# Encoder layer on one core: the sums move from GpSimd to VectorE, ten block pairs run two at a time, and six stores of the output add to a row stored early

## The chip, the cores and the metric

The kernel runs on one core of a Trainium2 chip. The metric is the device time of one execution in microseconds (us); the time before is the median of three runs. The engines are TensorE (PE, matrix products into PSUM), VectorE (DVE), ScalarE (ACT) and GpSimd (POOL); SyncE (SP) issues the transfers (DMA). SBUF is the on-chip memory, with 128 partitions.

## The reference

One encoder layer, S = D = 1024, float32. In short:

```python
h = x @ w_in
q, k, v, gate_a, alpha_low, pool_in, gate_b, merge_logits = split(h)
log_alpha = log_sigmoid(alpha_low @ w_alpha_up + b_alpha) / 16
o = gla_chunked(q * 128**-0.5, k, v, log_alpha)     # 4 heads, chunks of 64
y_a = (o * rsqrt(mean(o*o) + EPS) * gla_norm_g) * silu(gate_a)
y_b = (per-group (trailing mean - pool_in) @ w_pool_grp) * pool_scale * silu(gate_b)
g_a, g_b = split(sigmoid(merge_logits + b_merge))
y = (g_a * (y_a @ w_proj_a) + g_b * (y_b @ w_proj_b)) @ w_out
out = layernorm(2**0.25 * x + y, ln_g, ln_b)
```

## The kernel before

Every float32 operand is split into a hi and a lo part (float32r): ACT casts the hi part (L52), DVE subtracts it for the lo part (L53). A product of two operands is then three matmuls per 128 rows of depth.

Section A (0 to 378 us) projects q, k, v and the decay, and runs the four GLA heads, with PSUM pools ps_acc, ps_sc and ps_m of two tiles each. In `states` the running state st is updated by DVE (L427) from PSUM tiles ps_st, which come from ps_m; the scores ps_s come from ps_sc.

Section B (378 to 983 us) is 28 `Pair`s: pi0 to pi3 and gb0 to gb3 (the pooling branch and its gate), gta0 to gta3 (the gate of the GLA branch), lb0 to lb3 (a merge gate), pb and pa (the two output projections of the branches, 4 each), o0 to o3 (the last projection with the residual and the norm). The scratch products of `mix` and the norm have PSUM tiles of their own (ps_mx). Each Pair computes 256 output columns (or rows) by 1024 as a 2x2 block product with seven products instead of eight. A product is 12 matmuls of 128x512. The seven are 1 = B11, 7 = T3, 6 = T2, 5 = T1, 2 = B21, 4 = T4, 3 = B22, in the order "1765243"; T1 to T4 are sums of quarters of the moving operand, and products 7, 6, 5 and 3 need sums S of quarters of the weights. `prep` runs three products ahead of the matmuls (AHEAD): the sum S (L617, on POOL for pi, gb, gta and lb, on DVE for pb, pa and o), then the hi cast and the lo subtraction into a ring of four (whi, wlo). The products gather in PSUM banks a, b, c, d (psa_, psb_, psc_, psd_ with the Pair's name); DVE adds banks together (u at L645, e at L647) and `use` takes the four output tiles.

The sums T1 to T4 of an operand are made once (`Operands.ahead`, L196, eight instructions on POOL: ybp, yap, wop, xp), stored, and loaded and split by `make` when the operand is changed (`change`). WO's are made in the hooks of gta2 and gta3. In `gated` (pb, pa) the gate row is loaded, and POOL multiplies (L846) and adds (L848), but DVE in pa3. `norm_pair` normalises two rows of the output at a time: ACT scales, DVE multiplies with ln_g (L891), POOL adds ln_b (L892), SP stores. The last two rows go through `norm_one`.

Tiles are claimed from pools with few buffers, and a scheduler sets the order of the instructions on each engine; each engine then works in order.

Of the kernel before, what the change touches and what calls it, by code (L numbers as in the profile page):

```python
# [35 lines left out]
def encoder_layer(ctx: ExitStack, tc: tile.TileContext, xT, x, w_av, w_v, w_blk, w_up, b_al, g_norm,  # L36
# [147 lines left out]
    class Operands:  # L184
# [227 lines left out]
    def states(h):  # L412
# [4 lines left out]
        for b0 in range(0, NPR - 1, 2):  # L417
            ps = ps_m.tile([P, 512], F32, tag="m", name=f"ps_st{h}_{b0}")
# [91 lines left out]
    for h in range(H):  # L510
# [43 lines left out]
        f()  # L554
    fill(10400)
# [5 lines left out]
    c_v.release()  # L561
    ps_m.release()
# [19 lines left out]

    class Pair:


        def __init__(self, nm, fetch, operands, use, then=None, hooks=None, s_eng=pool_e, late=None, pre=None, order="1765243"):
            self.nm, self.fetch, self.operands, self.use, self.then = nm, fetch, operands, use, then
            self.hooks, self.s_eng, self.late = hooks or {}, s_eng, late
            self.w, self.s, self.ps = {}, {}, {}
            self.raw, self.load_next = None, 0  # L590
# [3 lines left out]
        def load(self):  # L594
            if self.raw is None:
                self.raw = []
                for i in range(2):
                    if self.nm == "o1" and i:
                        t = row(f"raw_{self.nm}_{i}")
                    else:  # L600
                        t = wraw.tile([P, 1024], F32, tag="raw", name=f"raw_{self.nm}_{i}")
                    with tc.high_priority(offset=200):
                        self.fetch(t, i)
                    self.raw.append(t)

        def quarter(self, q):
            return self.raw[int(q[0]) - 1][:, (int(q[1]) - 1) * 512:int(q[1]) * 512]

        def prep(self, i):
            p = self.products[i][0]  # L610
            q = self.quarter
            if i == 2 and self.late:
                self.late(self.raw)

            def total(a, b, op):
                t = sums.tile([P, 512], F32, tag="S", name=f"S{p}_{self.nm}")
                self.s_eng.tensor_tensor(out=t, in0=a, in1=b, op=op)  # L617
                self.s[p] = t
                return t
            src = {"1": lambda: q("11"), "2": lambda: q("12"), "4": lambda: q("22"),  # L620
                   "7": lambda: total(q("11"), q("21"), ALU.subtract),
                   "6": lambda: total(q("22"), self.s["7"], ALU.subtract),
                   "5": lambda: total(q("21"), q("22"), ALU.add),
                   "3": lambda: total(q("12"), self.s["6"], ALU.subtract)}[p]()
            self.w[i] = ring_split(src, f"{p}_{self.nm}", offset=0)

        def product(self, i):
            p, o, b, first = self.products[i]
            ps = self.ps
            if first:  # L630
                ps[b] = ps_st.tile([P, 512], F32, tag=b, name=f"ps{b}_{self.nm}", bufs=BANKS[b])
# [32 lines left out]
    def run(items, flat):  # L664
        pos = {id(it): n for n, it in enumerate(items)}
        items[0].load()
        for n in range(len(flat) + AHEAD):
            if n < len(flat):
                it, i = flat[n]
                if i == 0:  # L670
                    it.load()
                if i == it.load_next:
                    if pos[id(it)] + 1 < len(items):
                        items[pos[id(it)] + 1].load()
# [5 lines left out]
    def blk(w, j0):  # L680
        return lambda t, i: sp.dma_start(t.rearrange("p (a b) -> p a b", a=KB), w[j0 + i])
# [15 lines left out]
    def d_tile(nm):  # L697
# [352 lines left out]
```

## Time and profile before

| what | value |
|---|---|
| time, median of three runs (lowest to highest) | 1006.77 us (1003.89 to 1007.32) |
| the profiled execution's own time | 1002.75 us |
| its span in the trace | 1000.9 us |
| mean granted clock of TensorE, of full speed | 0.981 |
| busy: PE, DVE | 94%, 76% |
| busy: ACT, POOL | 40%, 34% |
| moved by DMA | 166 MB, 166 GB/s in the mean |

Busy time counts an engine's own instructions within the span of one profiled execution. An idle stretch of PE costs time; idle time of another engine costs only where PE waits behind it. A granted clock of 1.00 is 2.4 GHz, the lower level is 1.2 GHz.

### The profile page before, as it was taken

The numbers are of one execution on the slowest core, as the hardware profiler recorded it, in microseconds if no ns is written. First come the engines' busy times: TensorE is split into PE (matmuls) and PEld (weight loads), VectorE is DVE, ScalarE is ACT, GpSimd is POOL, SyncE is SP. The second block draws the span as 40 slices with busy tenths as digits, with TensorE's granted clock in tenths as the row PEclk, the third lists the DMA queues.
The fourth block names the chain that finished last, engine by engine and source line by source line (L and its number), as shares of the span: only waits on it lengthen the run. The fifth ranks groups of instructions, "written<-read, shape, count | busy, mean of one in ns | idle before, by whom it ended". The sixth has DMA issues, their size and how long they took to land. (4 is left out here: it accounts for less than half of the span.)

```text
span 1000.9 us, 13007 instructions
## 1 busy us (share of the span) xinstructions
PE 940.2 (94%) x4744; PEld 756.1 (76%) x4744; DVE 757.6 (76%) x1008; ACT 401.8 (40%) x673; POOL 344.1 (34%) x180
## 2 busy tenths in 40 slices
PE   9999799998999998999999999899999998988992
PEld 6887787786886885888888887678888876766772
DVE  5469959869776257767787768788886796689888
ACT  5255344253332225424333333233752552254552
POOL 1524323213213022222214367779111244510223
PEclk9999999899999999999999999999999999998997
DMA  8921120231123246121312497998987584499142
GB/s 281 334 93 34 33 72 31 75 112 37 49 91 84 85 121 231 43 94 64 116 59 79 137 344 294 326 328 325 381 291 249 214 323 160 168 296 303 43 147 84
DMA packets 74064, 165.99 MB, mean 166 GB/s; under 512 B 10336, under 2 KB 28000, under 8 KB 74000
## 3 DMA queue, kind: packets, MB, share of 16 engines
q1 hardware_dynamic: 74000, 165.16, 47.7%
q8 instruction: 37, 0.61, 0.3%
q14 instruction: 27, 0.22, 0.1%
HBM read 114.80 MB, written 50.33 MB: 165 GB/s over the span
## 5 line engine op out<-in xcount | busy, mean ns | idle before, releaser
L391 POOL TENSOR_TENSOR ks<-k,e 128x1024 f32<-128x1024 f32 x20 | 57.5, 2882 | 77.1 <-ACT e L387 67.5
L846 POOL TENSOR_TENSOR gpb<-tpb,gpb 128x512 f32<-128x512 f32 x12 | 21.7, 1812 | 87.3 <-DVE tpb L845 69.6
L122 PE MATMUL ps_la<-xl,whi_la 128*128 128x512 f32 x128 | 51.6, 403 | 0.0
L122 PE MATMUL ps_la<-xh,wlo_la 128*128 128x512 f32 x128 | 51.4, 402 | 0.0
L122 PE MATMUL ps_la<-xh,whi_la 128*128 128x512 f32 x128 | 51.1, 400 | 0.0
L387 ACT ACTIVATE e<-e 128x1024 f32<-128x1024 f32 x20 | 21.1, 1060 | 47.0 <-DVE e L386 47.0
L140 PE MATMUL ps_v<-whi_v,xh 128*128 128x264 f32 x128 | 37.0, 291 | 0.5 <-DVE k L288 0.5
L453 POOL TENSOR_TENSOR rsr_o<-rsa_o,mhalf 128x8 f32<-128x8 f32 x4 | 6.6, 1646 | 89.7 <-DVE rsa_o L452 89.7
L444 DVE COPY v<-ps_o 128x256 f32<-128x256 f32 x32 | 13.5, 421 | 31.1 <-PE ps_o L441 25.3
L140 PE MATMUL ps_v<-whi_v,xl 128*128 128x264 f32 x128 | 36.9, 289 | 0.0
L140 PE MATMUL ps_v<-wlo_v,xh 128*128 128x264 f32 x128 | 36.8, 291 | 0.0
L402 PEld LDWEIGHTS ps_s<-qs,ks 128*64 128x64 f32 x640 | 22.4, 139 | 14.7 <-issue 12.9
L390 DVE TENSOR_TENSOR qs<-q,e 128x1024 f32<-128x1024 f32 x20 | 30.2, 1510 | 3.2 <-ACT e L387 3.2
L320 POOL TENSOR_TENSOR ke<-k,e 128x1024 f32<-128x1024 f32 x4 | 12.0, 3004 | 56.2 <-DVE k L288 26.5
L402 PE MATMUL ps_s<-qs,ks 128*64 128x64 f32 x640 | 26.5, 228 | 4.5 <-DVE Pc L406 1.7
L453 POOL TENSOR_TENSOR rsr_ln<-rsa_ln,mhalf 128x2 f32<-128x2 f32 (+1 forms) x5 | 4.0, 811 | 74.5 <-DVE rsa_ln L452 74.5
L617 POOL TENSOR_TENSOR S_gb<-raw_gb,raw_gb 128x512 f32<-128x512 f32 x4 | 6.4, 1588 | 66.9 <-DMA raw_gb<-in_w_blk 51.5
L122 PEld LDWEIGHTS ps_la<-xh,whi_la 128*128 128x128 f32 x128 | 24.2, 189 | 5.9 <-issue 0.4
L122 PEld LDWEIGHTS ps_la<-xh,wlo_la 128*128 128x128 f32 x128 | 24.4, 190 | 5.4
L122 PEld LDWEIGHTS ps_la<-xl,whi_la 128*128 128x128 f32 x128 | 24.3, 190 | 5.4
L196 POOL TENSOR_TENSOR ybp<-ybp,ybp 128x1024 f32<-128x1024 f32 x8 | 22.0, 2750 | 15.7 <-DMA ybp<-yb 11.4
L445 ACT ACTIVATE ps_o<-v 128x256 f32<-128x256 f32 x32 | 12.4, 388 | 37.2 <-DVE v L444 37.2
(614 smaller groups left out, 3338.7 us busy)
## 6 DMA issues: line engine op xcount, KB each, us to landing
raw_v<-in_w_v SPq DMA_DIRECT2D x16, 264.0 KB, 2.6
xp<-in_xT SPq DMA_DIRECT2D x8, 512.0 KB, 6.8
oT<-oTs SPq DMA_DIRECT2D x32, 128.0 KB, 2.5
raw_la<-in_w_blk SPq DMA_DIRECT2D x8, 512.0 KB, 3.7
la<-la SPq DMA_DIRECT2D x8, 512.0 KB, 5.1
raw_pi<-in_w_blk SPq DMA_DIRECT2D x8, 512.0 KB, 4.2
raw_gb<-in_w_blk SPq DMA_DIRECT2D x8, 512.0 KB, 3.6
yb<-gb SPq DMA_DIRECT2D x16, 256.0 KB, 2.0
```

The costliest lines, as they stand in the source:

```text
L122: pe.matmul(ps[:, half * 512:half * 512 + 512], lhsT=a, rhs=mov(b, k, half), start=(i == 0), stop=(i == 23))
L140: pe.matmul(o, lhsT=sta(a, k, tb), rhs=w(k - k0)[b], start=(k == 0 and i == 0), stop=(k == KB - 1 and i == 2))
L196: pool_e.tensor_tensor(out=q[out_], in0=q[a], in1=q[b], op=op)
L320: pool_e.tensor_tensor(out=ke, in0=k, in1=e1, op=ALU.mult)
L387: act.activation(e, e, AF.Exp, scale=1.0 / TAU)
L390: dve.tensor_tensor(out=qs, in0=qt[h], in1=e, op=ALU.mult)
L391: pool_e.tensor_tensor(out=ks, in0=kt_[h], in1=e, op=ALU.mult)
L402: pe.matmul(psv[c * CH:c * CH + CH, b, :], lhsT=ks[:, cs], rhs=qs[:, cs], start=True, stop=True)
L444: dve.tensor_copy(v[b][:, hs], po)
L445: act.activation(po, v[b][:, hs], AF.Square, accum_out=d["ss"][:, b:b + 1])
L453: pool_e.tensor_tensor(out=r, in0=a, in1=mhalf[:, :w], op=ALU.pow)
L846: eng.tensor_tensor(out=o, in0=t, in1=o, op=ALU.mult)
```

## The change

- The weight sums of pi, gb, gta and lb (64), the sums of `ahead` for YB and YA (16) and WO (8), and the gate products of pb and pa (33) go from POOL to DVE. Weights come in quarters of 128x512 (`quart`, 8 buffers, loaded LEAD = 4 products ahead), and sums are made in place.
- WO's sums are made at the end of section A. The quarters pi and gta run in the orders 0, 1, 3, 2 and 0, 2, 1, 3.
- pi0 and gb0 run product by product in turn, with B11 and B21 first; so do, in the usual order, lb2/lb3, pb0/pb1, pb2/pb3, pa0/pa1, pa2/pa3 and o0/o1 (`both`).
- Banks a to d have two tiles each; ps_mx is gone, and its uses take banks b and d in turn (`spare`).
- Gates of pb and pa come in half rows, four of them; pa2 and pa3 keep their gate rows, from which DVE copies two weight quarters of o0 and o1.
- In `states`, the tiles from b0 = 4 on come from ps_sc.
- `bias_out` (at pi1's first product) stores ln_b into the row blocks 0, 4, 1, 5, 2 and 6 of the output; later, the stores of these blocks add to it (`accum_op`, on POOL's queue), and POOL's addition of ln_b is gone. Rows 3 and 7 both take the short form of `norm_one`.

```diff
+        def ahead(self, g, piece, eng):
...
-                pool_e.tensor_tensor(out=q[out_], in0=q[a], in1=q[b], op=op)
+                eng.tensor_tensor(out=q[out_], in0=q[a], in1=q[b], op=op)
...
-            ps = ps_m.tile([P, 512], F32, tag="m", name=f"ps_st{h}_{b0}")
+            ps = (ps_m.tile([P, 512], F32, tag="m", name=f"ps_st{h}_{b0}") if b0 < 4 else
+                  ps_sc.tile([P, 512], F32, tag="sc", name=f"ps_st{h}_{b0}"))
...
+    for g in range(2):
+        WO.ahead(g, lambda n, nm: gla.tile([P, 2, 512], F32, tag={"22": "KET", "12": "q", "11": "k", "21": "G"}[n], name=nm,
+                                           bufs=1 if n == "22" else 2), dve)
     fill(10400)
...
+        def loads(self, i):
+
+            qs = {"1": ("11",), "7": ("21",), "6": ("22",), "2": ("12",)}.get(self.products[i][0], ())
+            return [(q, self.late.get(q, LEAD)) for q in qs]
...
         def prep(self, i):
+            p, q = self.products[i][0], self.q
+            if p in "7653":
+                a, b, op, o = {"7": ("11", "21", ALU.subtract, "11"), "6": ("22", "11", ALU.subtract, "11"),
+                               "5": ("21", "22", ALU.add, "21"), "3": ("12", "11", ALU.subtract, "12")}[p]
+                dve.tensor_tensor(out=q[o], in0=q[a], in1=q[b], op=op)
...
+    def bias_out():
+
+        t = row("lnb_out")
+        sp.dma_start(t, ln_b.partition_broadcast(P))
+        for tb in (0, 4, 1, 5, 2, 6):
+            sp.dma_start(out[tb * P:tb * P + P, :], t)
...
-                eng.tensor_tensor(out=o, in0=t, in1=o, op=ALU.mult)
+                dve.tensor_tensor(out=o, in0=t, in1=o, op=ALU.mult)
...
-        dve.tensor_tensor(out=z[t], in0=z[t], in1=ln["g"], op=ALU.mult)
-        eng.tensor_tensor(out=z[t], in0=z[t], in1=ln["b"], op=ALU.add)
-        sp.dma_start(out[t * P:t * P + P, :], z[t])
+        for i in range(2):
+            dve.tensor_tensor(out=z[t][:, hs_[i]], in0=z[t][:, hs_[i]], in1=ln["g"][i], op=ALU.mult)
+        pool_e.dma_start(out[t * P:t * P + P, :], z[t], accum_op=ALU.add)
...
+    def both(a, b):
+        return [(it, i) for i in range(7) for it in (a, b)]
+
+    flat = [(it, i) for it in items[:2] for i in range(2)] + [(it, i) for it in items[:2] for i in range(2, 7)]
+    flat += [(it, i) for it in items[2:n] for i in range(7)]
+    for j in range(n, len(items), 2):
+        flat += both(items[j], items[j + 1])
+    flat += both(outs[0], outs[1]) + [(it, i) for it in outs[2:] for i in range(7)]
```

What stands on DVE before, in the first gta pairs (bank sums u and e, output tiles L766, products with the GLA output L806, lo parts of weights and of their sums S):

```order
L53 TENSOR_TENSOR wlo_gta_5046<-S_gta_5043,whi_gta_5045 128x512
L766 TENSOR_TENSOR gta_0_5021<-psd_gta_4985,u_gta_4920 128x512
L53 TENSOR_TENSOR wlo_gta_5076<-S_gta_5073,whi_gta_5075 128x512
L806 TENSOR_TENSOR gta_0_5021<-oTl_5063,gta_0_5021 128x1024
L806 TENSOR_TENSOR gta_1_4998<-oTl_5068,gta_1_4998 128x1024
L53 TENSOR_TENSOR wlo_gta_5115<-raw_gta_0_4829,whi_gta_5114 128x512
```

And in the same place of the changed kernel, the end of gta0 (L789 is the last step of gb2's mix, L619 the weight sums, L197 the sums of `ahead`, here of YB):

```order
L789 SCALAR_TENSOR_TENSOR gb_1_4663<-ps_mx_1_4762,psc_t,gb_1_4663 128x512
L53 TENSOR_TENSOR wlo_gta_4857<-raw_gta_4666,whi_gta_4856 128x512
L53 TENSOR_TENSOR wlo_gta_4879<-raw_gta_4772,whi_gta_4878 128x512
L619 TENSOR_TENSOR raw_gta_4772<-raw_gta_4772,raw_gta_4814 128x512
L619 TENSOR_TENSOR raw_gta_4814<-raw_gta_4814,raw_gta_4833 128x512
L768 TENSOR_TENSOR gta_1_4873<-psd_gta_4860,e_gta_4853 128x512
L53 TENSOR_TENSOR wlo_gta_4898<-raw_gta_4772,whi_gta_4897 128x512
L619 TENSOR_TENSOR raw_gta_4772<-raw_gta_4833,raw_gta_4772 128x512
L197 TENSOR_TENSOR ybp_0_4794<-ybp_0_4794,ybp_0_4796 128x1024
L768 TENSOR_TENSOR gta_1_4873<-psc_gta_4820,u_gta_4792 128x512
L53 TENSOR_TENSOR wlo_gta_4917<-raw_gta_4772,whi_gta_4916 128x512
L197 TENSOR_TENSOR ybp_0_4796<-ybp_0_4796,ybp_0_4798 128x1024
```

The sums that stood on POOL now stand between the lo parts and the output tiles, and the first sum of YB stands eight rows behind the mix that writes its input.

POOL's last instructions before (L453 is a power, L892 the addition of ln_b):

```order
L453 TENSOR_TENSOR rsr_ln_7712<-rsa_ln_7711,mhalf 128x2
L892 TENSOR_TENSOR z_7601<-z_7601,lnb 128x1024
L892 TENSOR_TENSOR z_7597<-z_7597,lnb 128x1024
L453 TENSOR_TENSOR rsr_ln_7863<-rsa_ln_7862,mhalf 128x2
L892 TENSOR_TENSOR z_7754<-z_7754,lnb 128x1024
L892 TENSOR_TENSOR z_7750<-z_7750,lnb 128x1024
L453 TENSOR_TENSOR rsr_ln_8048<-rsa_ln_8047,mhalf 128x2
L892 TENSOR_TENSOR z_7943<-z_7943,lnb 128x1024
L892 TENSOR_TENSOR z_7939<-z_7939,lnb 128x1024
```

And in the changed kernel (L902 issues the stores that add, L455 is the power):

```order
L455 TENSOR_TENSOR rsr_ln_7842<-rsa_ln_7841,mhalf 128x2
L455 TENSOR_TENSOR rsr_ln_7894<-rsa_ln_7893,mhalf 128x2
L902 DMA out<-z_7642 128x1024
L902 DMA out<-z_7638 128x1024
L902 DMA out<-z_7669 128x1024
L902 DMA out<-z_7665 128x1024
L455 TENSOR_TENSOR rsr_ln_8079<-rsa_ln_8078,mhalf 128x2
L902 DMA out<-z_7979 128x1024
L902 DMA out<-z_7975 128x1024
L455 TENSOR_TENSOR rsr_ln_8199<-rsa_ln_8198,mhalf 128x1
```

In place of each addition on POOL stands the issue of a store; the powers of the last rows have only these issues ahead of them.

## Rows read from the trace of the kernel before

**Rows 1.** The page's first part: busy time of PE in us, its share of the span, instructions; the same of the other engines.

```profile
PE 940.2 (94%) x4744; PEld 756.1 (76%) x4744; DVE 757.6 (76%) x1008; ACT 401.8 (40%) x673; POOL 344.1 (34%) x180
```

**Rows 2.** Busy time by stage: the stretch in us and its length, busy us and instructions of each engine, the mean granted clock of PE (1.00 is full), the busy share of the DMA engines and what they moved in GB/s.

```profile
100.00:200.00 100.00, 90.52 (x734) 77.80 (x733) 85.51 (x131) 36.56 (x61) 31.81 (x12) 0.97 0.19 53
300.00:378.00 78.00, 75.80 (x431) 60.99 (x429) 37.20 (x64) 19.13 (x37) 14.32 (x8) 0.98 0.32 93
378.00:400.00 22.00, 18.02 (x70) 12.37 (x69) 16.75 (x17) 13.21 (x17) 6.74 (x4) 1.00 0.69 263
400.00:550.00 150.00, 150.00 (x648) 121.59 (x647) 113.45 (x138) 53.60 (x101) 42.62 (x28) 1.00 0.22 76
600.00:650.00 50.00, 43.91 (x182) 34.57 (x181) 39.97 (x33) 16.86 (x29) 38.81 (x19) 0.97 0.85 310
650.00:700.00 50.00, 48.51 (x209) 39.03 (x208) 44.06 (x33) 18.74 (x30) 43.97 (x21) 1.00 0.89 326
800.00:950.00 150.00, 135.93 (x559) 107.04 (x559) 122.60 (x164) 67.65 (x104) 49.11 (x27) 0.97 0.65 218
950.00:983.20 33.20, 32.12 (x132) 23.97 (x131) 29.11 (x53) 16.97 (x38) 8.08 (x5) 1.00 0.33 111
983.20:1000.90 17.70, 0.00 (x0) 0.00 (x0) 13.45 (x24) 3.00 (x3) 7.57 (x4) 0.61 0.29 119
```

**Rows 3.** What PE waited for: the tile it was to write or read, what released it; us in all, times, the longest.

```profile
PE ps_st L422 <- DVE st L427: 7.4, 4, 2.6
PE psc_o L638 <- ACT whi_o L52: 4.5, 1, 4.5
PE psc_gta L638 <- DVE e_gta L647: 4.3, 1, 4.3
...
PE ps_o L439 <- DVE st L427: 1.9, 1, 1.9
```

**Rows 4.** The timeline from 623 to 643 us, of POOL, DVE and PE: start in us, duration (of all, where a row holds several), engine, line, operation, output and inputs, and in brackets the idle time ahead of it and what ended it.

```profile
623.14 11.44 POOL L196 TENSOR_TENSOR wop<-wop,wop 128x1024 f32<-128x1024 f32 x4
...
627.08 2.44 DVE L806 TENSOR_TENSOR gta<-oTl,gta 128x1024 f32<-128x1024 f32 x1 [3.38 <-DMA oTl<-oT]
629.44 2.89 DVE L53 TENSOR_TENSOR wlo_gta<-raw_gta,whi_gta 128x512 fp32r<-128x512 f32 x1
632.25 3.41 DVE L806 TENSOR_TENSOR gta<-oTl,gta 128x1024 f32<-128x1024 f32 x1
635.59 0.68 DVE L53 TENSOR_TENSOR wlo_gta<-raw_gta,whi_gta 128x512 fp32r<-128x512 f32 x1
...
639.26 0.77 PE L638 MATMUL psc_gta<-xT4h,whi_gta 128*128 128x512 f32 x1 [4.28 <-DVE e_gta L647]
...
640.25 0.63 PE L638 MATMUL psc_gta<-xT4h,wlo_gta 128*128 128x512 f32 x1
640.68 0.63 PE L638 MATMUL psc_gta<-xT4h,whi_gta 128*128 128x512 f32 x1
...
642.37 0.39 PE L638 MATMUL psc_gta<-xT4l,whi_gta 128*128 128x512 f32 x1
```

**Rows 5.** Groups of POOL's and DVE's instructions over the whole span: line, operation, shapes, count; busy us and mean ns of one; idle time ahead of them and what ended it.

```profile
L196 POOL TENSOR_TENSOR ybp<-ybp,ybp 128x1024 f32<-128x1024 f32 x8 | 22.0, 2750 | 15.7 <-DMA ybp<-yb 11.4 <-issue 4.1
L846 POOL TENSOR_TENSOR gpb<-tpb,gpb 128x512 f32<-128x512 f32 x12 | 21.7, 1812 | 87.3 <-DVE tpb L845 69.6 <-DMA yaT<-yaT_1d 13.5 <-DMA yaB<-ya 3.2
...
L617 POOL TENSOR_TENSOR S_gta<-raw_gta,raw_gta 128x512 f32<-128x512 f32 x4 | 5.8, 1450 | 24.0 <-DMA raw_gta<-in_w_blk 24.0
...
L53 DVE TENSOR_TENSOR wlo_lb<-raw_lb,whi_lb 128x512 fp32r<-128x512 f32 x12 | 20.8, 1737 | 2.9 <-ACT whi_lb L52 2.9
L806 DVE TENSOR_TENSOR gta<-oTl,gta 128x1024 f32<-128x1024 f32 x8 | 20.6, 2610 | 6.9 <-DMA oTl<-oT 6.9
L53 DVE TENSOR_TENSOR wlo_lb<-S_lb,whi_lb 128x512 fp32r<-128x512 f32 x16 | 20.2, 1262 | 3.7 <-ACT whi_lb L52 3.6
...
L53 DVE TENSOR_TENSOR wlo_pb<-S_pb,whi_pb 128x512 fp32r<-128x512 f32 x16 | 10.8, 681 | 0.0
```

**Rows 6.** The timeline of the tail, columns as in rows 4.

```profile
985.16 6.08 POOL L892 TENSOR_TENSOR z<-z,lnb 128x1024 f32<-128x1024 f32 x2 [5.12 <-DVE z L891]
...
987.97 3.82 DVE L917 SCALAR_TENSOR_TENSOR z<-z,mv,lng 128x512 f32<-128x512 f32 x2
...
991.21 1.53 POOL L453 TENSOR_TENSOR rsr_ln<-rsa_ln,mhalf 128x1 f32<-128x1 f32 x2
...
993.54 1.41 DVE L920 SCALAR_TENSOR_TENSOR z<-z,rsr_ln,lnb 128x512 f32<-128x512 f32 x2
...
996.12 1.23 DVE L892 TENSOR_TENSOR z<-z,lnb 128x1024 f32<-128x1024 f32 x1
997.37 0.33 SPq L893 DMA_DIRECT2D out<-z  x1
```

**Rows 7.** Transfers, grouped: destination and source, count, KB each, median us from issue to landing.

```profile
m<-gpa SPq DMA_DIRECT2D x16, 256.0 KB, 3.4
...
gpa<-la SPq DMA_DIRECT2D x8, 512.0 KB, 6.7
...
out<-z SPq DMA_DIRECT2D x7, 512.0 KB, 2.6
```

More of the change, by code (lines that the diff above doesn't have):

```diff
@@ L30 @@
 AHEAD = 3
+LEAD = 4
 ALPHA = 2.0 ** 0.25
@@ L587, in __init__ @@
             self.nm, self.fetch, self.operands, self.use, self.then = nm, fetch, operands, use, then
-            self.hooks, self.s_eng, self.late = hooks or {}, s_eng, late
-            self.w, self.s, self.ps = {}, {}, {}
-            self.raw, self.load_next = None, 0
+            self.hooks, self.late = hooks or {}, late or {}
+            self.w, self.ps, self.q = {}, {}, {}
             self.pre = pre
             self.products = [next(p for p in PRODUCTS if p[0] == n) for n in order]
[L594 to L604, printed above, removed]
@@ L630, in product @@
             if first:
[L631 removed]
+                ps[b] = bank(f"ps{b}_{self.nm}", b)
             whi, wlo = self.w.pop(i)
@@ L662, in product, with run @@
                 f()
-    def run(items, flat):
-        pos = {id(it): n for n, it in enumerate(items)}
-        items[0].load()
+    def run(flat):
+        begin = {}
+        for n, (it, i) in enumerate(flat):
+            for q, ahead_by in it.loads(i):
+                begin.setdefault(max(n - ahead_by, 0), []).append((it, q))
         for n in range(len(flat) + AHEAD):
+            for it, q in begin.get(n, ()):
+                it.load(q)
             if n < len(flat):
                 it, i = flat[n]
[L670 to L674, printed above, removed]
                 it.prep(i)
@@ L767, in use @@
                 act.activation(o, o, func, **kw)
-        return Pair(nm, blk(w_blk, j0), X, use, lambda: then(t), hooks)
+        return Pair(nm, blk(w_blk, j0), X, use, lambda: then(t), hooks, order="1276543" if nm == "gb0" else "1765243")
     def mix(gi, p):
@@ L778, in then @@
                 for half in range(2):
-                    ps = ps_mx.tile([P, 512], F32, tag="mx", name=f"ps_mx{j}_{half}")
+                    ps = bank(f"ps_mx{j}_{half}", next(spare))
                     n = 0
@@ L789, in mix @@
         return then
-    for gi in range(4):
+    for gi in (0, 1, 3, 2):
         pair, p = pool_pair(gi)
@@ L808, in y_a @@
         return then
-    more = [ahead(YB, 0), ahead(YB, 1), ahead(WO, 0), ahead(WO, 1)]
-    for q in range(4):
-        items.append(gate_pair(f"gta{q}", 8 + 2 * q, AF.Silu, y_a(2 * q), hooks=more[q]))
+    more = [ahead(YB, 0), None, ahead(YB, 1), None]
+    for n, q in enumerate((0, 2, 1, 3)):
+        items.append(gate_pair(f"gta{q}", 8 + 2 * q, AF.Silu, y_a(2 * q), hooks=more[n]))
     def keep(j0):
@@ L876, in residual @@
     def residual(tb):
-        if not ln:
-            for nm, src in (("g", ln_g), ("b", ln_b)):
-                ln[nm] = row(f"ln{nm}")
-                sp.dma_start(ln[nm], src.partition_broadcast(P))
         z[tb] = row(f"z_{tb}")
@@ L900, in norm_pair @@
             for half in range(2):
-                junk = ps_mx.tile([P, 512], F32, tag="mx", name=f"junk_{tb}{i}{half}")
+                junk = bank(f"junk_{tb}{i}{half}", next(spare))
                 act.activation(junk, z[tb + 4 * i][:, hs_[half]], AF.Square, bias=nm[:, i:i + 1], accum_out=ss[:, i, half:half + 1])
@@ L968, in use @@
                     sm.append(small(f"sm_{tb}", [2, 2], "sm"))
-                junk = ps_mx.tile([P, 512], F32, tag="mx", name=f"junk_{tb}{i}{half}s")
+                junk = bank(f"junk_{tb}{i}{half}s", next(spare))
                 act.activation(junk, o, AF.Identity, scale=-1.0 / D, accum_out=sm[0][:, i, half:half + 1])
```

175 lines of the change are left out of this document (82 added, 93 removed).

## The prediction

> **What bounds the kernel now.** I read the page's busy times first. TensorE (PE) is busy 940.2 of 1000.9 us and VectorE (DVE) 757.6 [rows 1], so time can come only from the 60.7 us in which PE is idle, unless matmuls run below full speed. The table by stage says where those 60.7 us lie [rows 2]: 9.48 at 100 to 200 us (the GLA heads), 3.98 at 378 to 400 (start of the pairs), nothing at 400 to 550, 6.09 + 1.49 at 600 to 700, 14.07 at 800 to 950, 17.7 in the tail after the last matmul. The stretch 400 to 550 also gives full speed: 648 matmuls in 150 us, 0.2315 us each, 2.78 us for a product of 12 and 19.4 for a pair of seven.
>
> The waits say what ended the idle time [rows 3]: nearly always a DVE instruction, or a hi cast on ScalarE (ACT) behind one. In section A it is the state update (st), at 639 us a sum of two banks (e_gta), at 901 the cast of the first weights of o0/o1 (whi_o).
>
> The timeline at 623 to 643 us [rows 4] shows why DVE is late though only three quarters busy. GpSimd (POOL) runs four sums from 623.14 to 634.58. Two DVE instructions beside them take 2.89 and 3.41 us. The first operation takes 0.68 right after they end; the second, on a tile twice as long, should take about 1.36. They lose 2.2 + 2.0 us, and PE's wait is the 4.28 us at 639.26. Afterwards matmuls stand 0.43 us apart (640.25 to 640.68), and seven of them fill 639.26 to 642.37, 3.1 us instead of 1.6: the granted clock, 0.97 in the mean of this stage [rows 2], was at 1.2 GHz and returned to 2.4. So a stall of 4.3 us costs some 1.5 us more.
>
> The groups say it over the run [rows 5]: wlo_lb takes 1737 and 1262 ns, where the same subtraction in pb, with POOL all but idle, takes 681; gta<-oTl takes 2610. POOL's own prices for the work in question are 1450 to 1812 ns a half tile and 2750 a whole one.
>
> **The change part by part**, against the profiled execution's own 1002.75 us (span 1000.9). The three timed runs have their median 4.02 us, or 0.4%, above it; I scale at the end.
>
> Section A. States 4 to 6 get their bank from ps_sc, so the two ps_m banks are not waited for a second time. The waits on st are 7.4 + 1.9 us [rows 3]. The scores now share ps_sc, so I take −5; bounds 0 and −9.3. WO's eight sums now run here on DVE: 8 × 1.36 = 11 us, where DVE is 37.2 of 78 us busy [rows 2]. Hidden, up to +4 if DVE blocks on a late load.
>
> Start of the pairs. pi0 and gb0 alternate, with B11 and B21 (resident since section A) first, so the first T operand is needed four products in, 11 us later than now. That covers nearly all of the 3.98 us: −3.5 (bounds 0 and −4.0).
>
> 600 to 700 us. No sum of POOL remains beside DVE. The idle is 7.58 us and the lost clock 1.5; I take −8.5 (bounds −3 and −9.1).
>
> 800 to 950 us. Two pairs at once double the time between a product and the next use of its bank or sum, from 2.78 to 5.6 us, and the resident gate rows of pa2/pa3 give o0/o1 their first weights without a store and a load behind the last product. Idle is 14.07 us; a mean clock of 0.97 over 150 us [rows 2] is up to 4.5 us more, of which I count 3.5, since the clock was low in part of the idle time itself. Of 17.6 I take −13 (bounds −6 and −17.6): the link from pa3 to o0 stays a chain through DVE.
>
> DVE's new load. Moved to it in the pairs: 64 weight sums and 33 gate operations of 128x512, and 16 sums of 128x1024. At 681 ns, and twice that, 43.6 + 22.5 + 21.8 = 88 us. What leaves with POOL is the slowing: wlo_lb 12 × 1.06 + 16 × 0.58 and gta 8 × 1.25 are 32 us in three groups alone. So DVE reaches about 814 us, still below PE. By stage: at 400 to 550 it has 113.45 us, and POOL's 28 instructions add 19: 132.5 of 150 even if nothing gets shorter. At 650 to 700 it has 33 instructions in 44.06 us, and POOL's 21, counted at 0.68, add 14: 58 of 50 if nothing gets shorter. But 33 in 44.06 is 1.34 each; all 54 at 0.68, and 0.68 more for each of up to 12 whole tiles among them, are 45. At 600 to 650 the three long DVE instructions of rows 4 alone give back 2.2 + 2.0 + 1.1. Hidden, but narrowly there.
>
> What I expect to go wrong, +6 (bounds 0 and +15). A DVE that does the sums itself waits in order for late weight quarters; POOL stood 24.0 us for raw_gta and 11.4 for ybp [rows 5] with no one behind it, now the next wlo and bank sums are queued behind. The order puts ybp's first sum eight instructions behind gb2's last mix, whose store and load must come between. In pa0/pa1 the four half-row slots are held for load, sigmoid, use and store. A 512 KB gate lands in 6.7 us and a 256 KB store in 3.4 [rows 7]; a slot is held at least some 8 us, two per use, four in all, against one use in 4 × 2.78 = 11 us. In o2/o3 the norm's scratch shares the banks b and d with the products. Each is a stall of 1 to 4 us; three of them make 6.
>
> bias_out. One load and six stores of 512 KB at the start of pi1, 2.6 us each alone [rows 7], some 18 us if nothing overlaps. They stand on SP's queue ahead of weight quarters, which have four products of lead and three of preparation, 19.5 us; DMA share is 0.22 there [rows 2]. Nothing, at most +3. The accumulating stores are on POOL's queue, which has only three small powers left there. o0's and o1's have until o3 needs rows 7 and 3, two at a time, over 10 us; o2's have o3's 19 us.
>
> The tail. Now: POOL adds ln_b to two rows from 985.16 to 991.24 [rows 6]; behind it POOL's power for the last two rows starts only at 991.21, and DVE's two subtractions beside it take 3.82 us. Then the last row goes through ACT, two DVE passes, the second of 1.23, and one store, to 1000.9. After: no add, and both rows take the short form. From the last matmul: bank add 0.7, statistics 0.7, aggregate and small ones 0.5, two subtractions with the power beside them 1.4, four small ones 0.6, four half-row passes (0.7 each) 2.8, then the store's 3.5 (997.37 to 1000.9) and gaps of about 0.5: 10.7 to 11 us instead of 17.7. −6.7 (bounds −3 and −8).
>
> Sum: −5 − 3.5 − 8.5 − 13 + 6 − 6.7 = −30.7: 972.0 own, and × 1006.77 / 1002.75 = **976 us**.
>
> A rule that speaks against the last part: the Trainium skill, SBUF — State Buffer, section "SBUF: two separate sides", says that a DMA issued from GpSimd needs GpSimd to write its descriptors, and that it is starved while DVE holds the port that both share. No row of this trace shows such a store, since all its transfers are SP's. By that rule the six stores would be late; what that costs is the last rival.
>
> **The rivals.**
> *The gain is half eaten* (985 to 1003). DVE is the new bound in one stage: if little there gets shorter, 600 to 700 keeps its 8.5 us (the 58 of 50 above), and blocked loads bring +15 instead of +6: 976 + 8.5 + 9 = 993. For it: DMA shares of 0.85 and 0.89 [rows 2], at which quarters can come late. Against it: WO's 16 transfers of 512 KB leave that stretch, and rows 4 show the slowing end with POOL.
>
> *The change does not do what it says* (within 0.3%). The stalls are then set by the loads, not by POOL or by DVE: each moves to the next instruction that waits, and the tail's 6.7 us are lost to one or two new stalls. Against it: in rows 3 no wait of PE is ended directly by a transfer.
>
> *Slower: the accumulating stores* (1010 to 1040). Rows 7 and 3 of o3 take the slots of rows 0 and 4, which come free only when these stores have landed. Up to some 6 us each nothing happens. At 20 us each, o2's pair, issued about 8 us into o3, ends 20 us behind the last matmul's 11, and o3 waits some 25 for its residual rows besides: 976 + 25 + 20 = 1021. It decides from about 15 us each. The Trainium skill, Collectives: The Full Stack, section "The bandwidth ceiling", has an addition on the way read two sources, so twice the read traffic; by that, as an estimate, twice 2.6 us, and nothing is lost. For the rival: DVE is 29.11 of 33.2 us busy from 950 on [rows 2], and a queue nobody used before is untried. Against it: 20 us is eight times the plain store.
>
> **How the numbers follow.** A difference of 0.3% is about what a measurement of this kernel tells from none. Forecast 0.52, own range 958 to 988. Half eaten 0.24. No net change 0.09. Slower by the stores, or by a DVE that blocks in several stages at once, 0.13. Below 957, if new stalls are absent and every term meets its bound, 0.02. The range 957 to 1006 leaves out the slower case and the last. Faster is 0.52 + 0.24 + 0.02 = 0.78.
>
> **What would show it.** Right: no idle over 1 us at 600 to 700; wlo_gta and wlo_lb near 0.7 us; PE idle below 5 us at 800 to 950; the tail at 10 to 12 us; DVE above 800 us. Wrong: PE waits on raw quarters, on half-row gates or on z rows; DVE at 95% in a stage with PE idle beside it; stores from POOL that take over 15 us.

## The result, and the profile after

The changed kernel takes 976.48 us (median of four runs, 972.46 to 978.98), the kernel before 1005.33 us in the same comparison: a ratio of 0.9709, interval 0.9667 to 0.9751. The forecast was 976 us. The profiled execution of the changed kernel has a span of 973.6 us and 975.38 us of its own time, 27.4 us under that of before, where the sum had −30.7. In the comparison of runs the gain is 28.9 us where the forecast had 30.8; that the two times agree to 0.5 us comes in part from the kernel before, which took 1005.33 us here and 1006.77 in the runs that the forecast started from.

Busy time first, as in [rows 1]:

```profile
PE 932.1 (96%) x4744; PEld 755.8 (78%) x4744; DVE 750.7 (77%) x1144; ACT 399.8 (41%) x676; POOL 111.4 (11%) x59
```

DVE does 136 instructions more and is busy 7 us less. By stage, with the columns of [rows 2]:

```profile
100.00:200.00 100.00, 88.99 (x717) 77.98 (x716) 84.96 (x131) 36.67 (x61) 29.55 (x12) 0.95 0.19 53
200.00:300.00 100.00, 95.21 (x658) 79.21 (x656) 71.89 (x125) 38.48 (x75) 26.49 (x10) 1.00 0.28 87
...
378.00:400.00 22.00, 21.06 (x91) 16.49 (x90) 17.59 (x23) 14.88 (x22) 0.00 (x0) 1.00 0.71 263
400.00:550.00 150.00, 149.69 (x646) 120.86 (x644) 119.01 (x169) 52.02 (x100) 0.00 (x0) 1.00 0.29 100
...
600.00:650.00 50.00, 50.00 (x217) 40.31 (x216) 41.96 (x56) 19.36 (x33) 0.00 (x0) 1.00 0.87 306
650.00:700.00 50.00, 50.00 (x218) 40.51 (x217) 37.59 (x52) 24.38 (x37) 0.00 (x0) 1.00 0.76 277
...
850.00:900.00 50.00, 42.18 (x164) 32.52 (x165) 47.96 (x83) 23.72 (x32) 0.00 (x0) 0.90 0.82 278
900.00:950.00 50.00, 48.23 (x207) 38.52 (x207) 38.56 (x76) 31.22 (x70) 5.57 (x6) 1.00 0.41 97
```

600 to 700 us has no idle time of PE left, where [rows 2] had 7.58. 378 to 400 went from 3.98 to 0.94. One large stall stands at 850 to 900, with the clock at 0.90. Section A is no better: 11.0 us idle at 100 to 200 and 4.8 at 200 to 300. What PE waits for, as in [rows 3]:

```profile
PE psb_o L634 <- ACT whi_o L52: 6.3, 2, 6.1
PE ps_o L441 <- ACT P L410: 4.0, 1, 4.0
PE ps_o L441 <- DVE P L411: 3.4, 2, 2.7
PE ps_v L141 <- DVE v L149: 3.1, 1, 3.1
PE ps_s L403 <- DVE egl L307: 2.6, 2, 1.3
```

None of them is for a sum of banks, and none for the state st. The groups that answer to [rows 5], and the transfers that answer to [rows 7] (the six accumulating stores stand last, on POOL's queue):

```profile
L53 DVE TENSOR_TENSOR wlo_lb<-raw_lb,whi_lb 128x512 fp32r<-128x512 f32 x28 | 19.2, 684 | 6.2 <-ACT whi_lb L52 6.2
...
L808 DVE TENSOR_TENSOR gta<-oTl,gta 128x1024 f32<-128x1024 f32 x8 | 9.8, 1223 | 3.7 <-DMA oTl<-oT 3.4
L197 DVE TENSOR_TENSOR ybp<-ybp,ybp 128x1024 f32<-128x1024 f32 x8 | 9.8, 1222 | 2.6 <-DMA ybp<-yb 2.5
```

```profile
out<-lnb_out SPq DMA_DIRECT2D x6, 512.0 KB, 5.0
...
out<-z POOLq DMA_DIRECT2D x6, 512.0 KB, 5.7
```

wlo_lb fell from 1737 and 1262 ns to 684, gta<-oTl from 2610 to 1223. The tail, as in [rows 6]; the last matmul ends at 962.97:

```profile
962.52 1.40 DVE L926 SCALAR_TENSOR_TENSOR z<-z,mv,lng 128x512 f32<-128x512 f32 x2
963.84 0.68 DVE L959 TENSOR_TENSOR z<-psd_o,z 128x512 f32<-128x512 f32 x1
...
965.76 1.06 POOL L455 TENSOR_TENSOR rsr_ln<-rsa_ln,mhalf 128x1 f32<-128x1 f32 x1 [2.06 <-DVE rsr_ln L460]
...
966.99 1.41 DVE L929 SCALAR_TENSOR_TENSOR z<-z,rsr_ln,lnb 128x512 f32<-128x512 f32 x2
```

It takes 10.6 us instead of 17.7. Three stretches, cut at the first matmul of pi0 and the end of the last matmul, say where the 27.3 us of span came from:

| stretch | before | after | difference | in the sum |
|---|---|---|---|---|
| section A | 375.9 | 375.8 | −0.1 | −5 |
| the pairs | 607.3 | 587.2 | −20.1 | −3.5 − 8.5 − 13 + 6 = −19 |
| tail | 17.7 | 10.6 | −7.1 | −6.7 |

### The profile page after: what moved, and what is told of

Read it like the earlier page. It is cut to its first block, busy times and chain, and to the rows that moved or that the text cites. A ratio compares the mean times of both kernels' runs of the same rounds, so it can differ in the third digit from the quotient of the medians.

```text
span 973.6 us, 13056 instructions
## 1 busy us (share of the span) xinstructions
PE 932.1 (96%) x4744; PEld 755.8 (78%) x4744; DVE 750.7 (77%) x1144; ACT 399.8 (41%) x676; POOL 111.4 (11%) x59
## 5 line engine op out<-in xcount | busy, mean ns | idle before, releaser
L455 POOL TENSOR_TENSOR rsr_ln<-rsa_ln,mhalf 128x2 f32<-128x2 f32 (+1 forms) x5 | 5.1, 1014 | 583.0 <-PE psc_o L634 571.0
L52 ACT CAST whi_gb<-raw_gb 128x512 fp32r<-128x512 f32 x28 | 17.3, 621 | 49.0 <-PE psd_pi L634 14.8
L391 DVE TENSOR_TENSOR qs<-q,e 128x1024 f32<-128x1024 f32 x20 | 33.5, 1674 | 2.1 <-ACT e L388 2.0
L52 ACT CAST whi_lb<-raw_lb 128x512 fp32r<-128x512 f32 x28 | 17.4, 621 | 37.1 <-PE psd_lb L634 9.3
L52 ACT CAST whi_gta<-raw_gta 128x512 fp32r<-128x512 f32 x28 | 17.3, 618 | 33.9 <-PE psd_gta L634 10.1
L52 ACT CAST whi_pi<-raw_pi 128x512 fp32r<-128x512 f32 x28 | 17.4, 620 | 32.6 <-PE psd_gb L634 7.0
L52 ACT CAST whi_pb<-raw_pb 128x512 fp32r<-128x512 f32 x28 | 17.1, 619 | 32.8 <-PE psd_pb L634 11.2
L141 PEld LDWEIGHTS ps_v<-whi_v,xh 128*128 128x128 f32 x128 | 25.3, 198 | 4.5 <-DVE v L149 3.4
L52 ACT CAST whi_o<-raw_o 128x512 fp32r<-128x512 f32 x28 | 16.9, 617 | 25.1 <-DVE raw_o L619 8.8
```

The lines of the kernel that those rows point to most:

```text
L52: act.copy(hi, src)
L141: pe.matmul(o, lhsT=sta(a, k, tb), rhs=w(k - k0)[b], start=(k == 0 and i == 0), stop=(k == KB - 1 and i == 2))
L391: dve.tensor_tensor(out=qs, in0=qt[h], in1=e, op=ALU.mult)
L455: pool_e.tensor_tensor(out=r, in0=a, in1=mhalf[:, :w], op=ALU.pow)
```

## The experiments

**The engines alone.** In the kernel before, only the engine of the sums and gate operations:

```diff
-        def __init__(self, nm, fetch, operands, use, then=None, hooks=None, s_eng=pool_e, late=None, ...
+        def __init__(self, nm, fetch, operands, use, then=None, hooks=None, s_eng=dve, late=None, ...
...
+            eng = pool_e if self.nm == "x" else dve
-                pool_e.tensor_tensor(out=q[out_], in0=q[a], in1=q[b], op=op)
+                eng.tensor_tensor(out=q[out_], in0=q[a], in1=q[b], op=op)
...
-                             dve if q == 3 else pool_e)
+                             dve)
```

> The kernel before, with only the engine changed: weight sums, the sums of `ahead` for YB, YA and WO and the gate operations on DVE; loads, banks, order of the pairs and the stores as before. Theory 1 (the prediction: POOL beside DVE is what makes DVE late): wlo_gta and wlo_lb at 0.68 to 0.72 us, DVE's busy time within 10 us of the 757.6 before though it does 121 instructions more in the pairs, the idle of 7.6 us at 600 to 700 falls below 2, and the time falls by 7 to 12 us, to 993 to 998. Theory 2 (DVE is full: what it gains per instruction it spends on the added ones, and it now waits in order for late weights and sums of WO): 600 to 700 keeps 4 us of idle or more, and the time is within 4 us of before or above it.

Measured: 989.14 us against 1005.18, ratio 0.9856 (0.9813 to 0.9899), −16 us and more than theory 1 asked. DVE is busy 758.3 us with 121 instructions more. The stages of [rows 2] in which POOL worked hardest:

```profile
600.00:650.00 50.00, 50.00 (x217) 40.58 (x216) 43.38 (x58) 18.48 (x31) 0.00 (x0) 1.00 1.01 365
650.00:700.00 50.00, 50.00 (x218) 40.63 (x217) 38.47 (x54) 22.05 (x34) 0.00 (x0) 1.00 0.95 356
```

All 7.58 us of idle are gone from these two stretches, though the DMA engines are busy 1.01 and 0.95 of the time: transfers were not what set these stalls. Over 545 to 715 us, 2.6 us of idle are left, at 562 and 596. More than half of the whole gain is this move.

**Which of POOL's work it was.** In the changed kernel, first the 64 weight sums back on POOL, then only the 16 sums of YB and YA:

```diff
-                dve.tensor_tensor(out=q[o], in0=q[a], in1=q[b], op=op)
+                (pool_e if self.nm[:2] in ("pi", "gb", "gt", "lb") else dve).tensor_tensor(out=q[o], in0=q[a], in1=q[b], op=op)
```

> The changed kernel, with only the 64 weight sums of pi, gb, gta and lb back on POOL. Theory 1 (POOL beside DVE slows both): the 28 wlo of lb and of gta take 0.9 us or more in the mean instead of 0.68, 4 us or more of idle come at 545 to 715, and the time rises by 5 to 12 us. Theory 2 (DVE's own load is what counts; 64 instructions less help as much as the slowing costs): within 3 us of the changed kernel.

```diff
-        return {0: [lambda: ops.ahead(g, lambda n, nm: c4.tile([P, 2, 512], F32, tag="c", name=nm), dve)]}
+        return {0: [lambda: ops.ahead(g, lambda n, nm: c4.tile([P, 2, 512], F32, tag="c", name=nm), pool_e)]}
```

> The changed kernel, with only the 16 sums of YB and YA (128x1024, four in a row) back on POOL. Theory 1 (the stall at 639 us of the kernel before came from four long sums in a row on POOL, so it is these and not the 64 weight sums that slow DVE too much): single wlo and gta<-oTl beside them take 2.4 to 3.4 us again, PE idles for 2 us or more at 545 to 715, and the time rises by 3 to 8 us. Theory 2 (with quarters, spread loads and no other work on POOL, DVE has slack enough to take the slowing): PE's idle at 545 to 715 stays below 1.5 us and the time within 2 us of the changed kernel.

Measured: 979.12 us (975.71 to 983.79) and 976.61 us (974.13 to 979.04); neither differs from the changed kernel by more than the runs scatter. The slowing is there: the first line is of the version with the weight sums on POOL, the others of the one with YB's and YA's, where two wlo beside four long sums take 3.50 us and one sum 2.78.

```profile
L53 DVE TENSOR_TENSOR wlo_lb<-raw_lb,whi_lb 128x512 fp32r<-128x512 f32 x28 | 23.7, 846 | 11.1 <-ACT whi_lb L52 11.1
```

```profile
574.10 11.00 POOL L197 TENSOR_TENSOR ybp<-ybp,ybp 128x1024 f32<-128x1024 f32 x4 [219.20 <-DMA ybp<-yb]
...
579.33 3.50 DVE L53 TENSOR_TENSOR wlo_gta<-raw_gta,whi_gta 128x512 fp32r<-128x512 f32 x2
582.87 2.78 DVE L619 TENSOR_TENSOR raw_gta<-raw_gta,raw_gta 128x512 f32<-128x512 f32 x1
```

So slowing alone is not a stall. PE's idle at 545 to 715 rises only from 0.6 to 1.5 us in the second. In the kernel before, the weight sums and those of YB, YA and WO came together; put back alone, neither the weight sums nor those of YB and YA use up what DVE has in hand. That it takes several groups at once is not shown: both groups together, WO's sums and the gate operations were not put back.

**Two pairs at once.** lb2 to pa3, the ten of the title, one after another again (pi0/gb0 and o0/o1 still go in twos):

```diff
-        flat += both(items[j], items[j + 1])
+        flat += [(it, i) for it in items[j:j + 2] for i in range(7)]
```

> The changed kernel, with lb2 to pa3 one after another instead of two at once; o0/o1 and pi0/gb0 stay as they are. Theory 1 (the prediction: the distance between a product and the next use of its bank or sum is what takes the stalls out at 790 to 870): waits of 1 to 4 us on bank sums and wlo come back in pa, and the time rises by 4 to 8 us, to 980 to 985. Theory 2 (the stalls there were POOL's gate operations and full DVE queues, gone with the move): within 2 us of the changed kernel.

Measured: 986.24 us, ratio to before 0.9824 (0.9787 to 0.9860), 9.8 us above the changed kernel and a little more than theory 1 had. The waits it named are back, and the one at o0 grows from 6.1 to 7.9:

```profile
PE psb_o L634 <- ACT whi_o L52: 7.9, 1, 7.9
...
PE psc_pa L634 <- ACT whi_pa L52: 3.6, 1, 3.6
...
PE psc_pa L634 <- DVE e_pa L643: 2.6, 1, 2.6
```

This is what two at once gives within the changed kernel, not against the one before. From the first matmul of pi0 to the end of the last, the kernel before takes 607.3 us, the one with the engines alone, whose pairs also run one after another, 591.7, the changed kernel 587.2 and this version 599.0. PE's waits in pa are 6.3 us before and 2.1 with the engines alone; the longest of before, and the longest that the engines alone leave:

```profile
PE psc_pa L638 <- DVE e_pa L647: 3.3, 1, 3.3
```

```profile
PE psa_pa L639 <- ACT u_pa L644: 1.8, 1, 1.8
```

So theory 2 holds for the stalls of the kernel before. The rest of the change brings waits of its own when the pairs run one after another, 7.3 us, and two at once takes out these and 4.5 us more. Which part brings them was not tested.

**The PSUM tiles of the states.** Undone in the changed kernel, and done alone in the one before (the same two lines, either way):

```diff
-            ps = (ps_m.tile([P, 512], F32, tag="m", name=f"ps_st{h}_{b0}") if b0 < 4 else
-                  ps_sc.tile([P, 512], F32, tag="sc", name=f"ps_st{h}_{b0}"))
+            ps = ps_m.tile([P, 512], F32, tag="m", name=f"ps_st{h}_{b0}")
```

> The changed kernel, with all PSUM tiles of `states` from ps_m again. Theory 1 (the prediction's term: the second use of a ps_m bank is what st is waited for): section A, from the start to the first matmul of pi0, gets 4 to 6 us longer than the changed kernel's 375.8 us, and waits of ps_st on st come back with 5 us or more. Theory 2 (the term was empty: section A is held by a chain of DVE, ACT and POOL in each head, and whatever bank is freed, the wait is taken at the next matmul of the chain): section A stays within 2 us of 375.8, with waits under other names, and the time within 0.3%.

> The kernel before, with only the PSUM tiles of `states` from b0 = 4 on taken from ps_sc. Theory 1: section A 4 to 6 us shorter than 375.9 us, the time 0.4 to 0.6% lower. Theory 2: section A within 2 us, the time within 0.3%; the waits of ps_st on st go, waits of ps_o or ps_s on P, Pc or egl come.

Measured: undone, 976.72 us and a section A of 377.4 us; alone, 999.49 us, ratio 0.9947 (0.9925 to 0.9970), and a section A of 371.3. Alone it gives the 5 us of the term. Undone it costs nothing that can be seen: the time is the same, and 377.4 lies among the 374.7 to 377.8 us of the seven versions whose section A is that of the changed kernel. Yet the waits on st are back:

```profile
PE ps_st L423 <- DVE st L428: 8.0, 4, 2.8
```

The waits of the version with the change alone are those of the changed kernel, a little shorter:

```profile
PE ps_o L440 <- ACT P L409: 3.5, 1, 3.5
...
PE ps_o L440 <- DVE P L410: 2.4, 1, 2.4
...
PE ps_s L402 <- DVE egl L306: 1.4, 2, 1.2
```

Both theories hold in part: the waits on st turn into others, as theory 2 says, but shorter ones. Something else in the changed section A takes it back.

**WO's sums.** Back in the hooks of gta2 and gta3, still on DVE:

```diff
-    for g in range(2):
-        WO.ahead(g, lambda n, nm: gla.tile([P, 2, 512], F32, tag={"22": "KET", "12": "q", "11": "k", "21": "G"}[n], name=nm,
-                                           bufs=1 if n == "22" else 2), dve)
...
-    more = [ahead(YB, 0), None, ahead(YB, 1), None]
+    more = [ahead(YB, 0), ahead(WO, 0), ahead(YB, 1), ahead(WO, 1)]
```

> The changed kernel, with WO's sums back in the hooks of gta2 and gta3 (on DVE, as YB's). Theory 1 (the sums in section A eat what the PSUM tiles of `states` give): section A 2 to 4 us shorter than 375.8, near the 371.3 of the kernel before with the PSUM change alone; 600 to 700 carries 10 us of DVE and 16 transfers more and gets 1 to 4 us of idle; the time within 3 us of the changed kernel. Theory 2 (section A has the waits of a new order whatever WO does): section A within 1 us of 375.8.

Measured: 971.48 us (971.07 to 972.44), ratio to before 0.9660 (0.9635 to 0.9685), 5 us under the changed kernel. Section A takes 372.8 us; 600 to 700 idles 0.52 us. The waits of section A:

```profile
PE ps_o L441 <- ACT P L410: 3.3, 1, 3.3
...
PE ps_o L441 <- DVE P L411: 2.4, 1, 2.4
PE ps_s L403 <- DVE egl L307: 1.4, 2, 1.2
```

These three are 2.9 us shorter together than in the changed kernel. Three versions without WO's sums in section A (this one and the last two below) take 371.6 to 372.8 us for it, the seven with them 374.7 to 377.8. So the sums cost some 3.5 us there, most of what the tiles had given, and nothing that can be seen in gta. How they cost it is open. In the changed kernel they run from 326 to 343 us, DVE waits 5.7 us for their loads, and PE 0.7 for DVE. But of the 3.0 us between the two traces 2.3 are there when the first of these loads is issued, at 247.7 us, and up to there the named instructions of the engines stand in the same order in both.

**The accumulating stores.** Without bias_out; ln_b added by POOL, or by DVE, in half rows and stored by SP, the short form of the last rows kept:

```diff
-        pool_e.dma_start(out[t * P:t * P + P, :], z[t], accum_op=ALU.add)
+        for i in range(2):
+            pool_e.tensor_tensor(out=z[t][:, hs_[i]], in0=z[t][:, hs_[i]], in1=ln["b"][i], op=ALU.add)
+        sp.dma_start(out[t * P:t * P + P, :], z[t])
```

> The changed kernel without bias_out, with ln_b added by POOL in half rows and stored by SP; the short form of both last rows stays. Theory 1 (the prediction: POOL's adds stand ahead of the last powers): the tail after the last matmul is 4 to 7 us longer than the changed kernel's 10.7, and the time 4 to 8 us above it. Theory 2 (the tail was shortened by the short form alone): within 2 us of the changed kernel.

> The changed kernel without bias_out, with ln_b added by DVE in half rows (12 instructions of 0.68 us more) and stored by SP. Theory 1 (what the adding stores save is POOL's slowing of DVE: beside POOL's adds three wlo took 4.0 us instead of 1.9): no DVE instruction of o2 and o3 is slowed, the 8 us more of DVE cost 1 to 5 us, and the time lies between the changed kernel and the 988 of the version with the adds on POOL, at 977 to 982. Theory 2 (what costs is the store on SP's queue, ahead of which nothing else gets through, or any add at all): 985 or more.

Measured: 988.19 us (ratio to before 0.9813, 0.9778 to 0.9849) and 983.86 us (0.9785, 0.9755 to 0.9814), 11.7 and 7.4 us above the changed kernel. Yet the tail does not grow: it takes 9.8 us with the adds on POOL, whose last add ends at 972.98, ahead of the last matmul's end at 976.8. What grows is o2 and o3. With the adds on POOL, three wlo beside them take 4.03 us, and PE waits 4.2 us for one of them:

```profile
946.54 6.73 POOL L903 TENSOR_TENSOR z<-z,lnb 128x512 f32<-128x512 f32 x4 [5.12 <-DVE z L901]
...
970.09 2.89 POOL L903 TENSOR_TENSOR z<-z,lnb 128x512 f32<-128x512 f32 x2 [0.63 <-DVE z L901]
```

```profile
950.39 4.03 DVE L53 TENSOR_TENSOR wlo_o<-raw_o,whi_o 128x512 fp32r<-128x512 f32 x3
```

In the changed kernel the same three take 1.89:

```profile
945.49 1.89 DVE L53 TENSOR_TENSOR wlo_o<-raw_o,whi_o 128x512 fp32r<-128x512 f32 x3
```

With the adds on DVE nothing is slowed, but 8.2 us more of DVE's work in o2 and o3 cost 7.4. It came between the two theories' numbers; the waits (psd_o on z, 4.8 us, psa_o on wlo_o, 3.7) are DVE's, which speaks for the added work and against SP's queue. Part of both losses is the clock behind the waits: from 950 us to the last matmul its mean is 0.75 with the adds on POOL, 0.85 on DVE and 1.00 in the changed kernel.

**The stall at o0.** In the changed kernel at 880 to 890 us, ACT, DVE and PE:

```profile
884.60 1.04 ACT L52 CAST woB21h<-woB 128x1024 fp32r<-128x1024 f32 x1 [1.99 <-DMA woB<-in_w_o]
887.47 1.04 ACT L52 CAST woT4h<-woT 128x1024 fp32r<-128x1024 f32 x1 [1.83 <-DMA woT<-woT_0d]
888.42 0.61 ACT L52 CAST whi_o<-raw_o 128x512 fp32r<-128x512 f32 x1
```

```profile
883.78 0.36 DVE L942 COPY raw_o<-gpa 128x128 f32<-128x128 f32 x2
885.67 1.22 DVE L53 TENSOR_TENSOR woB21l<-woB,woB21h 128x1024 fp32r<-128x1024 f32 x1 [1.54 <-ACT woB21h L52]
886.82 2.49 DVE L619 TENSOR_TENSOR raw_o<-raw_o,raw_o 128x512 f32<-128x512 f32 x4
```

```profile
889.09 0.79 PE L634 MATMUL psb_o<-woT2h,whi_o 128*128 128x512 f32 x1 [6.09 <-ACT whi_o L52]
```

The weights of o0's product 6 are copied by 884.1, but their sum waits on DVE behind the lo part of B21, and their cast on ACT behind B21 and T4, all for loads that come late and are needed later. So the four operands were made later:

```diff
+        to_wo = change(YA, WO)
+        late_wo = {n: to_wo.pop(i) for n, i in ((0, 3), (2, 4), (3, 5), (4, 6))}
-        items.append(gated(f"pa{q}", 2 * q, YA, w_pa, gate_a, mb_d, to_dram, change(YA, WO) if q == 3 else None, keep=q > 1))
+        items.append(gated(f"pa{q}", 2 * q, YA, w_pa, gate_a, mb_d, to_dram, to_wo if q == 3 else None, keep=q > 1))
...
-        return Pair(f"o{tb}", fetch, WO, use, done, late={"22": 1} if tb < 2 else None, pre=pre, ...
+        return Pair(f"o{tb}", fetch, WO, use, done, late_wo if tb == 1 else None, late={"22": 1} if tb < 2 else None, pre=pre, ...
```

> The changed kernel, with WO's last four operands (T1, B21, T4, B22) made in the hooks of o1's products 0, 2, 3 and 4 instead of pa3's 3 to 6, so that the casts and subtractions of the weights for product 6 of o0 and o1 stand ahead of those of B21 and T4 on ACT and DVE. Theory 1 (the changed kernel's longest wait, 6.1 us at 889, is one of queues: whi_o is behind the casts of woB21 and woT4, which wait for loads that land at 884.6 and 887.5): the wait falls to 3 us or less, and the time by 3 to 5 us, to 971 to 974. Theory 2 (the chain from pa3's last product over gates, sums and copies on DVE is that long by itself): product 6 starts within 1.5 us of 889, or what is gained is waited for again at B21; the time within 2 us of the changed kernel.

Measured: 973.6 us (971.02 to 974.72), ratio to before 0.9676 (0.9648 to 0.9705), 2.9 us under the changed kernel, whose runs (972.46 to 978.98) overlap with these. The wait is 1.0 us in two; another of 2.6 came up, on a bank that b shares with the norm's scratch:

```profile
PE psb_o L634 <- ACT junk L914: 2.6, 1, 2.6
...
PE psb_o L634 <- ACT whi_o L52: 1.0, 2, 0.6
```

From o0's first matmul to the end of the last it is 87.0 us instead of 91.3.

**Both together, and the scratch elsewhere.** The edits of the last experiment and of WO's sums in one kernel; then also the norm's scratch in an SBUF tile:

```diff
-                junk = bank(f"junk_{tb}{i}{half}", next(spare))
+                junk = post.tile([P, 512], BF16, tag="jk", name=f"junk_{tb}{i}{half}", bufs=1)
```

> The changed kernel with both gains at once: WO's sums in the hooks of gta2 and gta3, and WO's last four operands made in o1's hooks. Theory 1 (they lie in different stages and add): 5 and 3 us below the changed kernel, 967 to 970. Theory 2 (the second takes place in a stretch that the first makes tighter): 971 or more.

> As a_best, with the norm's scratch results (which nobody reads) in one SBUF tile instead of the banks b and d. Theory 1 (the banks shared with the norm cost what the prediction feared: 2.6 us of psb_o behind ACT's junk, and product 2 moved ahead of 6 in o2 and o3): another 2 to 4 us less, 964 to 967. Theory 2 (the wait is ACT's queue, and a bank wait only hides it): within 1.5 us of a_best.

Measured: 968.31 us (967.08 to 970.37), ratio to before 0.9632 (0.9605 to 0.9659): the two gains add, 8.2 us under the changed kernel and 3.2 under WO's sums alone, clear of the scatter of either. With the scratch in SBUF it is 973.34 us (969.21 to 976.65), 5 us worse: the wait on the bank goes, one of 4.9 us on z (psd_o) comes in o3, and the tail takes 14.3 us instead of 10.6. Behind the wait on z DVE stands for the residual rows of o3, whose loads on SP's queue waited for the accumulating stores (first row DVE's, second SP's waits):

```profile
949.33 0.69 DVE L951 SCALAR_TENSOR_TENSOR z<-z,u_o 128x512 f32<-128x512 f32 x1 [7.62 <-DMA z<-in_x]
```

```profile
SPq L884 <- DMA out<-z: 29.5, 2, 27.0
```

POOL issues the first two stores at 931.0 and 932.2 us, and at 925.4 and 927.2 with the scratch in the banks; the two loads behind them go out at 936.9 and 939.8 instead of 931.5 and 934.1. Why the norm comes later with the scratch in SBUF was not tested.

## Why the prediction was right, step by step

**600 to 700.** Right in place, cause and size. POOL's instructions beside DVE made DVE late, and moving them alone empties the stretch. The trace of the kernel before also shows which of DVE's instructions are slowed. Beside one sum of POOL, the instruction with an input in PSUM takes its 0.68 us, and the next, with both in SBUF, 2.30:

```profile
600.78 2.86 POOL L196 TENSOR_TENSOR ybp<-ybp,ybp 128x1024 f32<-128x1024 f32 x1
...
601.29 0.68 DVE L766 TENSOR_TENSOR gta<-psd_gta,u_gta 128x512 f32<-128x512 f32 x1
601.89 2.30 DVE L53 TENSOR_TENSOR wlo_gta<-S_gta,whi_gta 128x512 fp32r<-128x512 f32 x1
```

The Trainium skill, SBUF — State Buffer, section "Who interferes with whom", says that a DVE instruction with two SBUF inputs contends with a GpSimd instruction that reads SBUF. This trace agrees: of DVE's 128x512 TENSOR_TENSOR that overlap with one of POOL's, the 107 with all inputs in SBUF take 1.46 us in the mean, 0.68 without POOL; the 54 with an input in PSUM stay at 0.68.

**DVE's new load.** Right that it is hidden, too high in size: the sum had about 814 us busy, and above 800 as a sign of being right; measured 750.7. I had counted the slowing in three groups, 32 us. With the engines alone, 121 instructions more leave the busy time at 758.3 us against 757.6. By the prediction's prices these instructions are an estimated 99 us, its 88 and 11 for WO's sums; so about 98 us of slowing went with POOL.

**Section A.** This step failed: −5 forecast, −0.1 measured. The tiles alone do give 4.6 us of section A. The failure is the other half of that paragraph, WO's sums "hidden, up to +4": they cost some 3.5 us, near the upper bound. DVE does block on late loads there, as the bound supposed, but PE waits only 0.7 us for DVE in that time; how the rest comes about is open.

**Start of the pairs.** −3.5 forecast; the idle fell by 3.0 us. With the engines alone 3.91 us of it stay, so it is not POOL's work; the order of pi0 and gb0 was not tested by itself.

**800 to 950.** Right that a chain from pa3 to o0 stays, wrong in what makes up the gain. The sign was less than 5 us of idle here; 9.75 are left, 6.1 of them one stall at o0. The sum gave its 13 us to two pairs at once and the resident rows, but the engines alone bring the idle from 14.07 to 9.27, and the pairs as a whole down by 15.5 of the 20.1 us. Two at once is worth 9.8 us against waits that are in good part new. The stall that stayed is longer than it has to be, because of queues on ACT and DVE that I had not looked at.

**What I expected to go wrong.** Of the +6 little reached PE at the places named. DVE waited 2.5 us for ybp, 2.3 for a weight quarter and 2.1 for half rows, and no wait of PE followed. In o2/o3 late weights cost 1.3 and 0.4 us and a shared bank 0.9. The stall at o0 is of this kind all the same, work held up behind late loads on engines that work in order, at a place that the paragraph does not name.

**The tail.** Right in size, and in the main in the mechanism: POOL's last power ends 9.6 us behind the last matmul before (992.74 against 983.15) and 3.9 in the changed kernel (966.82 against 962.97). The other 1.4 us lie behind the power, where the second of the last rows takes the short form. But the accumulating stores are not needed for it: with the adds on POOL the tail is as short, since the norm of o2's rows stands earlier. Its power starts 3.8 us ahead of the last matmul's end before and 11.4 in the changed kernel, so the adds are done when the last power comes. The earlier norm and the short form were not tested apart. The accumulating stores have their worth earlier, in o2 and o3: 7 to 12 us against putting the adds back, for which the sum had no term.

**The rivals.** The half-eaten gain needed DVE's instructions to stay long; wlo_lb fell to 684 ns. The slower one did not come near in the changed kernel: the six stores land in 5.7 us in the median and 6.4 at most, plain ones of the same size in 5.0 in the same kernel and in 2.6 in [rows 7], the decision point was 15. Its mechanism is there all the same, and shows with the scratch in SBUF, where DVE waits 7.6 us for rows that these stores hold up. The starvation that the Trainium skill, SBUF — State Buffer, section "SBUF: two separate sides", describes is not seen at this size, with DVE 10.64 of 12 us busy from 950 on; the section says it of DVE in a two-port mode, and no run here shows whether an instruction beside these stores was in one. The twice read traffic of the prediction's estimate can't be told from these times either, since the plain stores of this kernel are nearly as slow.

**The sum.** The total is partly luck. Section A gave nothing where 5 us were forecast, the engines gave nearly twice the 8.5 us that the sum had for them, and two pairs at once went largely into what the rest of the change costs.

## What to carry to other kernels

Look at what runs beside a slow instruction before counting its engine as full: moving 121 instructions to DVE left its busy time as it was, because the engine they came from had been lengthening DVE's. Slowing alone is not yet a stall: each of the two groups that were put back alone was absorbed, so such a trial shows nothing. And a part that is taken out of the changed kernel is priced against the rest of the change, not against the kernel before: two pairs at once is worth 9.8 us there, and the engines alone already had most of what it was meant to save. Operands that are prepared early stand in front of what is needed first: order the casts by need, and look at which load the engine ahead of the critical one waits for.

## What the runs showed that I had not expected

Issuing an accumulating store holds POOL for 0.86 to 1.07 us (six, 5.4 us in all). And 8.2 us more of DVE's work in the last two pairs can cost 7.4, though even with them DVE is busy only 41.59 of 50 us there (900 to 950). The load that takes a stored tile next waits until the store has landed, too: with the norm's first stores some 5 us later, it came too late for DVE.
